# First layer's down projection: the last latent operands are split ahead of two closings, and the second layer's rows are loaded in other places

## The chip, the cores and the metric

One core of a Trainium2 chip runs the whole kernel. The metric is the device time of one execution in microseconds (us). Engine names in the profile: PE is the matrix engine (PEld its weight loads), DVE the vector engine, ACT the scalar engine, POOL GpSimd; SP only issues DMAs here, in a fixed order, and POOL issues the stores of results.

## The reference, cut to what matters

Two layers run over 1024 latent tokens and 256 context tokens, 1024 wide. Each layer has a mixer and a gated FFN with a convolution. The change lies where the FFN of the first layer ends and the mixer of the second begins:

```python
u = h @ w_up; u = conv3(u) + conv_b
a, g = jnp.split(u, 2, axis=-1)
y = (jax.nn.silu(g) * a) @ w_down            # 2816 x 1024, the "down projection"
x   = x   + g2  * rms_norm(y_lat, norm_post_ffn)      # "closing" of latent rows
ctx = ctx + g2c * rms_norm(y_ctx, norm_post_ffn)      # closing of context rows
...
h_lat = rms_norm(x, norm_pre_mix[1]) * (1.0 + sc1) + sh1   # second layer, mixer
qkv = h_lat @ w_qkv
```

## The kernel before, in words

Every float32 product is made of three matmuls on rounded halves: an operand is split by an ACT copy into a high part (`d_Ah`, `d_Bh`, line 1809) and by a DVE subtraction into a low part (`d_Al`, `d_Bl`, line 1810), and PE multiplies high by high, low by high, high by low (line 136, through the helper `mm`). A is the activation (`actd`), B the weight (`w_down`).

`ffn_down` (line 1750) runs in numbered steps `g`. Steps 0 to 41 are the latent tokens: seven products of a Strassen scheme, `P1, P5, P2, P3, P6, P4, P7`, of six chunks each (`NG` = 6, `NS` = 42; a chunk has 1024 columns, the sixth, that is step 41, only 512). P7 is special: at step 39 PE takes its last three chunks (steps 39, 40, 41) together, for one of the four result tiles after the other, so that all operands of steps 40 and 41 must be there soon after step 39 begins. For the first result tile these are 6 matmuls of step 39, 6 of step 40, then 3 of step 41. Steps 42 to 63 are the context tokens: one weight each, `k` = 0 to 21 (called weight 0 to 21 below), 512 KB each, 12 matmuls per weight; the last four weights, 18 to 21, are multiplied together at step 60. The activation of the context comes in pieces of four weights, the last piece is half as large (256 KB, with weight 20). Steps up to 71 follow without products.

In each step the program writes the products, then `prepare` (the operands of later steps: `prep`, and the loads of still later ones: `loads`), then the entries of `todo` for that step, and from step 42 on one `next(other)`. At step 39 (`last`) `prepare` comes first. This written order is the order of each engine's queue; no scheduler reorders it. A queue stands still while its first instruction waits.

- For latent operands of P7, `prep` first corrects the weight on DVE (`total`, line 1814: `d_t<-d_rawB,d_t`), ACT makes the high parts, DVE the low ones.
- `todo` holds the closings. `add(y2..)` adds a result bank to a saved tile (`p1`, line 1937: `y<-d_ps,d_p`). `leave(i)` closes 128 latent rows: two multiplications (line 1959), two additions of the old rows (line 1937: `y<-y,y_x`), two stores to `x2d` (POOL, line 1963). Latent tiles 4 to 7 are closed by `leave(4)` to `leave(7)` at steps 45, 47, 49, 51, with one store each (line 1965).
- `other` is the generator `odd_early` (line 2145): from a certain step on it writes one row load of the second layer per step (`odd_load`, line 2128: `n_x<-x2d`, 512 KB on SP; row tiles 0 to 7 below) and, from the third load on, one step of `odd_norm` for row tiles 0 to 3: a square with sum on ACT (line 2137), a power on POOL, a scaling on DVE (line 2140). A row tile gathers 8 tokens from each of 16 grid rows, so it needs every latent tile to be stored. First load: step 56; last: step 63.
- A weight's load (`d_rawB<-in_w_down`, line 1775, SP) goes to one of three buffers; weight k waits until weight k - 3 is split. At step g the load of weight g - 36 is written, just ahead of that step's `next(other)`.

After step 71 come the two context closings (`out`, `leave(8)`, `leave(9)`), then `odd_values` of the second layer (transposes of the rows, line 2190, and the first products `g_ps`); its weight loads (`w_raw<-in_w_qkv`, line 2170) stand on SP behind the row loads.

Of the kernel before, what the change touches and what calls it, by code (L numbers as in the profile page):

```python
# [65 lines left out]
class Trunk:  # L66
# [1683 lines left out]
    def ffn_down(self, l, ctx, x_src, x_dst, hp, sp, pp, tp, beside=None):  # L1750
# [9 lines left out]
        NG = (H + 1) // 2  # L1760
        width = lambda c: min(2, H - 2 * c)

        def tile(pool, tag, name, n=1024, dtype=F32, bufs=1):
            return pool.tile([P, n], dtype, name=name, tag=tag, bufs=bufs)
# [165 lines left out]
        def at(g, f):  # L1930
            todo.setdefault(g, []).append(f)

        def square(src, ms, h):
            nc.scalar.activation(junk, src, AF.Square, scale=1.0 / 32.0, accum_out=ms[:, h:h + 1])

        def add(out, x, y):
            nc.vector.tensor_tensor(out=out, in0=x, in1=y, op=OP.add)
# [3 lines left out]
        def fetch_x(key, r):  # L1941
            pool, tags = [(sp, ("f_t0",)), (sp, ("f_t1",))][key % 2] if key not in (4, 5) else \
                (sp, [("w_S1h", "w_S1l"), ("w_S2h", "w_S2l")][key - 4])
            if len(tags) == 1:
                x = tile(pool, tags[0], "y_x", NTOK if ctx else SEQ)
                st["x", key] = [x[:, 512 * h:512 * h + 512] for h in range(2)]
                nc.sync.dma_start(x[:, :D], x_src(r))
            else:
                st["x", key] = [tile(pool, t, "y_x", 512) for t in tags]
                for h, x in enumerate(st["x", key]):  # L1950
                    nc.sync.dma_start(x, x_src(r)[:, 512 * h:512 * h + 512])

        def scale(key, ms):
            st["r", key] = self.y_rstd(ms)

        def leave(key, halves, kind, r, whole=None):

            for h, y in enumerate(halves):
                nc.vector.scalar_tensor_tensor(out=y, in0=y, scalar=st["r", key], in1=gates[kind][h], op0=OP.mult, op1=OP.mult)
            for h, (y, x) in enumerate(zip(halves, st.pop(("x", key)))):  # L1960
                add(y, y, x)
                if whole is None:
                    nc.gpsimd.dma_start(x_dst(r)[:, 512 * h:512 * h + 512], y)
            if whole is not None:
                nc.gpsimd.dma_start(x_dst(r), whole)
# [20 lines left out]
        Y = [y01[:, :512], y01[:, 512:], y23[:, :512], y23[:, 512:]]  # L1986
# [4 lines left out]
        p1 = [tile(sp, "w_" + t, "d_p1", 512) for t in ("S1h", "S1l", "S2h", "S2l")]  # L1991
        y1a = [tile(self.wp, "w_" + t, "y", 512) for t in ("A12h", "A12l", "A21h", "A21l")]
        y1b = [tile(p, "w_" + t, "y", 512) for p, t in ((self.wp, "A22h"), (self.wp, "A22l"), (sp, "S3h"), (sp, "S3l"))]
        y2 = [tile(hp, "x_T4" + x, "y") for x in ("0h", "0l", "1h", "1l")]
        ms1, ms2 = ([self.small.tile([P, 2], F32, name=f"y_ms{j}", bufs=4) for _ in range(4)] for j in range(2))
        for i in range(4):
            at(NG + 1 + i, lambda i=i: nc.scalar.copy(p1[i], X[i]))
            at(2 * NG + 1 + i, lambda i=i: add(y2[i][:, 512:], Y[i], p1[i]))
            at(3 * NG + 1 + i, lambda i=i: (nc.scalar.copy(y1a[i], X[i]), square(X[i], ms1[i], 0)))
            at(4 * NG + 1 + i, lambda i=i: add(y1b[i], Y[i], p1[i]))  # L2000
            at(5 * NG + 1 + i, lambda i=i: add(y1b[i], X[i], y1b[i]))
            at(5 * NG + 2 + i, lambda i=i: square(y1b[i], ms1[i], 1))
            at(5 * NG + 3 + i, lambda i=i: scale(i, ms1[i]))
            at(6 * NG + 1 + i // 2 * (1 if ctx else 2), lambda i=i: add(y2[i][:, :512], Y[i], p1[i]))
        for i, (g, g1) in enumerate(((25, 34), (26, 35), (36, 38 if ctx else 39), (37, 39))):
            at(g, lambda i=i: fetch_x(i, i * P))
            at(g1, lambda i=i: leave(i, (y1a[i], y1b[i]), 0, i * P))
        r2 = lambda i: SEQ // 2 + i * P
# [54 lines left out]
        for i in range(5 if ctx else 0):  # L2063
            g = 6 * NG + 7 + 2 * i
# [80 lines left out]
    def odd_early(self, nx, junk):  # L2145

        self.odd_x = {}
        for _ in range(14):
            yield
        norm = self.odd_norm(range(4), junk)  # L2150
        for i in range(8):
            self.odd_load(nx, i)
            if i >= 2:
                next(norm)
            yield

    def odd_values(self, nx, gp, tp, sp):

# [643 lines left out]
```

## Time and profile before

| | us |
|---|---|
| runs before: median (lowest, highest of 3) | 3343.87 (3343.53, 3350.19) |
| the profiled execution: time | 3345.86 |
| the profiled execution: span of its instructions | 3344.1 |
| around the span | 1.8 |
| PE busy in the span | 3105.4 (93%) |
| mean granted clock of PE | 0.967 |

All times of the trace count from the start of the span. The down projection of the first layer lies between about 1675 and 1966 us, and the place of the change between 1870 and 1975 us. In a timeline row the first number is the start, the second the duration, then engine, line, operation and tiles; the bracket tells how long the engine was idle before it and what it waited for. A row of DMA issue tells when SP or POOL issued, not when the data landed; when a load landed is seen where an engine waited for it. Matmuls overlap, so a row of 0.39 us is followed by the next start 0.227 us later.

### The profile page before, as it was taken

To read this page: it belongs to the slowest core of one execution; us is meant where nothing else is said; L and a number is where in the kernel's file an instruction comes from. 1 tells how busy PE (TensorE), PEld (TensorE's weight loads), DVE (VectorE), ACT (ScalarE), POOL (GpSimd) and SP (SyncE) were. 2 spreads that over 40 slices of the span, in tenths; PEclk is the share of its full clock that TensorE was granted. 3 is DMA by queue.
4 is the path that set the end of the run, shared out by engine and by line. 5 is a ranking of instruction groups with operands and counts; after the bars stand their busy time and mean duration, and the time that the engine had idled before them with its cause. 6 is when DMAs were issued, how large, how long until landed. Compare 5 with 4: busy or idle time off the path is not lost.

```text
span 3344.1 us, 48796 instructions
## 1 busy us (share of the span) xinstructions
PE 3105.4 (93%) x18364; PEld 2555.0 (76%) x18364; DVE 2023.0 (60%) x3399; ACT 1501.9 (45%) x2681; POOL 1555.5 (47%) x1178
## 2 busy tenths in 40 slices
PE   7989998779998799999999989999998989999997
PEld 4766776658887688888878768889986768888785
DVE  4356666667775755455477863477775565545778
ACT  3222222266665544334344442466665534434443
POOL 1130111197774476666510111577774367777202
PEclk8999999889999899999999989999998989999998
DMA  6534333231113221122285772222224222222856
GB/s 247 195 90 138 123 120 115 88 97 45 59 67 126 71 72 66 70 74 70 80 297 191 256 242 105 79 65 62 61 74 161 85 69 76 88 82 82 277 182 220
DMA packets 202684, 398.73 MB, mean 119 GB/s; under 512 B 23360, under 2 KB 84800, under 8 KB 202448
## 3 DMA queue, kind: packets, MB, share of 16 engines
q1 hardware_dynamic: 191968, 358.91, 32.2%
q0 software_dynamic: 10480, 36.71, 2.9%
q8 instruction: 144, 2.36, 0.3%
q14 instruction: 92, 0.75, 0.1%
HBM read 316.86 MB, written 79.06 MB: 118 GB/s over the span
## 4 chain that ended last, share of the span: by engine, by line
PE 72%; DVE 10%; ACT 3%; issue 3%; DMA 3%; POOL 2%; SPq 0%; POOLq 0%; DVEq 0%; ACTq 0%
PE g_ps L136 18%; PE u_g L136 14%; PE u_v L136 10%; PE d_ps L136 10%; PE u_pc L136 4%; PE a_pv L136 2%; PE c_pv L136 2%; PE c_s L136 2%; PE c_pt L2437 2%; PE a_pt L1080 2%; DVE a_pl L1082 1%; PE o_ps L136 1%; PE a_s L136 1%; PE mod_ps L136 1%; ACT a_ph L1081 1%
## 5 line engine op out<-in xcount | busy, mean ns | idle before, releaser
L144 POOL TENSOR_TENSOR rs_r<-rs_e,mhalf 128x1 f32<-128x1 f32 (+3 forms) x106 | 82.2, 776 | 929.9 <-DVE rs_e L143 877.1
L136 PE MATMUL d_ps<-d_Bh,d_Ah 128*128 128x512 f32 x704 | 276.1, 392 | 7.4 <-ACT d_Bh L1809 7.3
L136 PE MATMUL d_ps<-d_Bl,d_Ah 128*128 128x512 f32 x704 | 276.7, 393 | 3.5 <-DVE d_Bl L1810 3.1
L136 PE MATMUL d_ps<-d_Bh,d_Al 128*128 128x512 f32 x704 | 275.9, 392 | 1.6 <-DVE d_Al L1810 1.6
L2420 POOL TENSOR_SCALAR c_p<-c_p,rl 128x640 f32<-128x640 f32 (+1 forms) x128 | 232.6, 1818 | 95.9 <-DVE rl L2419 63.7
L1060 POOL TENSOR_SCALAR a_p<-a_p,rl 128x1280 f32<-128x1280 f32 (+1 forms) x80 | 240.4, 3010 | 54.3 <-DVE rl L1059 47.1
L136 PE MATMUL g_ps<-xh,w_hi 128*128 128x512 f32 (+1 forms) x640 | 258.2, 403 | 3.6 <-DVE hq L711 2.2
L136 PE MATMUL g_ps<-xh,w_lo 128*128 128x512 f32 (+1 forms) x640 | 238.9, 373 | 0.9 <-POOL w_lo L2320 0.9
L136 PE MATMUL g_ps<-xl,w_hi 128*128 128x512 f32 (+1 forms) x640 | 239.1, 374 | 0.0
L1082 DVE TENSOR_TENSOR a_pl<-a_pt,a_ph 128x512 fp32r<-128x512 f32 (+1 forms) x200 | 119.0, 603 | 91.7 <-ACT a_ph L1081 91.6
L1497 DVE TENSOR_TENSOR f_u<-u_v,f_p 128x512 f32<-128x512 f32 x88 | 60.5, 688 | 186.2 <-PE u_v L136 186.2
L1483 POOL TENSOR_TENSOR w_S4l<-w_s,w_S4h 128x512 fp32r<-128x512 f32 x44 | 57.2, 1300 | 231.1 <-ACT w_S4h L1482 231.1
L136 PEld LDWEIGHTS d_ps<-d_Bh,d_Ah 128*128 128x128 f32 x704 | 133.1, 189 | 37.0 <-ACT d_Bh L1809 8.2
L136 PEld LDWEIGHTS d_ps<-d_Bl,d_Ah 128*128 128x128 f32 x704 | 133.1, 189 | 35.2 <-DVE d_Bl L1810 7.2
L136 PEld LDWEIGHTS d_ps<-d_Bh,d_Al 128*128 128x128 f32 x704 | 132.9, 189 | 30.1 <-DVE d_Al L1810 3.0
L136 PEld LDWEIGHTS g_ps<-xh,w_hi 128*128 128x128 f32 x640 | 122.6, 192 | 42.6 <-issue 27.7
L1081 ACT CAST a_ph<-a_pt 128x512 fp32r<-128x512 f32 (+1 forms) x200 | 101.9, 518 | 107.2 <-PE a_pt L1080 107.1
L136 PE MATMUL g_ps<-w_hi,xh 128*128 128x512 f32 (+1 forms) x368 | 144.2, 392 | 4.8 <-DVE xh L2194 2.1
L2440 DVE TENSOR_TENSOR c_pl<-c_pt,c_ph 128x256 fp32r<-128x256 f32 (+1 forms) x256 | 113.0, 470 | 58.3 <-ACT c_ph L2439 57.1
L136 PE MATMUL g_ps<-w_lo,xh 128*128 128x512 f32 (+1 forms) x368 | 137.9, 375 | 4.1 <-DVE w_lo L2181 2.9
L136 PEld LDWEIGHTS g_ps<-xh,w_lo 128*128 128x128 f32 x640 | 122.1, 191 | 23.9 <-POOL w_lo L2320 1.3
L2439 ACT CAST c_ph<-c_pt 128x256 fp32r<-128x256 f32 (+1 forms) x256 | 98.4, 414 | 91.2 <-PE c_pt L2437 89.1
(546 smaller groups left out, 9901.1 us busy)
## 6 DMA issues: line engine op xcount, KB each, us to landing
m_raw<-in_w_mod SPq DMA_DIRECT2D x96, 512.0 KB
w_raw<-in_w_up SPq DMA_DIRECT2D x88, 512.0 KB
d_rawA<-actd SPq DMA_DIRECT2D x77, 512.0 KB
d_rawB<-in_w_down SPq DMA_DIRECT2D x74, 512.0 KB
actd<-f_t SPq DMA_DIRECT2D x22, 640.0 KB
d_t<-in_w_down SPq DMA_DIRECT2D x22, 512.0 KB
actd<-f_t SPq DMA_DIRECT2D x22, 512.0 KB
d_s<-actd SPq DMA_DIRECT2D x20, 512.0 KB
```

The costliest lines, as they stand in the source:

```text
L136: return self.nc.tensor.matmul(out, lhsT, rhs, start=start, stop=stop, skip_group_check=True, **k)
L144: nc.gpsimd.tensor_tensor(out=r[:p, :n], in0=e[:p, :n], in1=self.mhalf[:p, :n], op=OP.pow)
L1060: nc.gpsimd.tensor_scalar(Pt[:, :nk], Pt[:, :nk], rl, None, op0=OP.mult)
L1080: nc.tensor.transpose(pt[:, m, qt * P:(qt + 1) * P], Pt[:, kts[j + m] * P:(kts[j + m] + 1) * P], self.ident)
L1081: nc.scalar.copy(ph[:, j:j + n], pt[:, :n])
L1082: nc.vector.tensor_tensor(out=pl[:, j:j + n], in0=pt[:, :n], in1=ph[:, j:j + n].bitcast(F32), op=OP.subtract)
L1483: nc.gpsimd.tensor_tensor(out=lo, in0=part(j, name), in1=hi.bitcast(F32), op=OP.subtract)
L1497: nc.vector.tensor_tensor(out=out, in0=x, in1=y, op=OP.add)
L2420: nc.gpsimd.tensor_scalar(Pt[:, :n], Pt[:, :n], rl, None, op0=OP.mult)
L2437: nc.tensor.transpose(pt[:, j, :], Pt[:, (src + j) * P:(src + j + 1) * P], self.ident)
L2439: nc.scalar.copy(vap(ph, o, dims), pt[:, :cnt])
L2440: nc.vector.tensor_tensor(out=vap(pl, o, dims), in0=pt[:, :cnt], in1=vap(ph, o, dims).bitcast(F32), op=OP.subtract)
```

## The change

```diff
-            at(6 * NG + 1 + i // 2 * (1 if ctx else 2), lambda i=i: add(y2[i][:, :512], Y[i], p1[i]))
-        for i, (g, g1) in enumerate(((25, 34), (26, 35), (36, 38 if ctx else 39), (37, 39))):
+            at(6 * NG + 1 + i // 2 * 2, lambda i=i: add(y2[i][:, :512], Y[i], p1[i]))
+        for i, (g, g1) in enumerate(((25, 34), (26, 35), (36, 39), (37, 39))):
...
-        for _ in range(14):
+        for _ in range(11):
             yield
         norm = self.odd_norm(range(4), junk)
         for i in range(8):
             self.odd_load(nx, i)
             if i >= 2:
                 next(norm)
             yield
+            if i < 6:
+                yield
```

`ctx` is true in the first layer alone; in the second layer nothing changes. In the first, two `add(y2..)` and `leave(2)` go from step 38 to step 39, where `prepare` stands ahead of `todo`. The row loads go from steps 56 to 63 to steps 53, 55, 57, 59, 61, 63, 65 and 66, and the norm's steps with the last six of them. No instruction is added or taken away.

On DVE, at the end of the latent products (`d_t`, `d_Al`, `d_Bl` with 512 columns are the operands of step 41; `y<-d_ps,d_p` the adds; the two multiplications with a gate and the `y<-y,y_x` pair behind them one `leave`). Before, from the last operand of step 40 on:

```order
L1810 TENSOR_TENSOR d_Bl<-d_t,d_Bh 128x1024
L1937 TENSOR_TENSOR y<-d_ps,d_p_16002 128x512
L1937 TENSOR_TENSOR y<-d_ps,d_p_16003 128x512
L1959 SCALAR_TENSOR_TENSOR y<-y,rs_r,gate_15996 128x512
L1959 SCALAR_TENSOR_TENSOR y<-y,rs_r,gate_15997 128x512
L1937 TENSOR_TENSOR y<-y,y_x 128x512 x2
L1814 TENSOR_TENSOR d_t<-d_rawB,d_t 128x512
L1810 TENSOR_TENSOR d_Al<-d_s,d_Ah 128x512
L1810 TENSOR_TENSOR d_Bl<-d_t,d_Bh 128x512
```

With the change, the same place:

```order
L1810 TENSOR_TENSOR d_Bl<-d_t,d_Bh 128x1024
L1814 TENSOR_TENSOR d_t<-d_rawB,d_t 128x512
L1810 TENSOR_TENSOR d_Al<-d_s,d_Ah 128x512
L1810 TENSOR_TENSOR d_Bl<-d_t,d_Bh 128x512
L1937 TENSOR_TENSOR y<-d_ps,d_p_16002 128x512
L1937 TENSOR_TENSOR y<-d_ps,d_p_16003 128x512
L1959 SCALAR_TENSOR_TENSOR y<-y,rs_r,gate_15996 128x512
L1959 SCALAR_TENSOR_TENSOR y<-y,rs_r,gate_15997 128x512
L1937 TENSOR_TENSOR y<-y,y_x 128x512 x2
```

The three operations of step 41 now stand ahead of the two adds and of `leave(2)`; `leave(3)`, which followed them before, stands behind all of it still. On POOL the order is the same as before.

On SP, at the last context weights (`d_rawB` with `x4` are weights 17 to 20 in the line taken out, `d_rawA` the last half-size piece, `n_x` the row loads):

```order
 L1775 DMA d_rawA<-actd 128x4x256
-L1775 DMA d_rawB<-in_w_down 128x1024 x4
-L1775 DMA d_rawA<-actd 128x2x256
+L1775 DMA d_rawB<-in_w_down 128x1024
+L2128 DMA n_x<-x2d 128x1x1024
+L1775 DMA d_rawB<-in_w_down 128x1024 x2
 L2128 DMA n_x<-x2d 128x1x1024
 L1775 DMA d_rawB<-in_w_down 128x1024
-L2128 DMA n_x<-x2d 128x1x1024 x3
+L1775 DMA d_rawA<-actd 128x2x256
+L1775 DMA d_rawB<-in_w_down 128x1024
+L2128 DMA n_x<-x2d 128x1x1024 x2
```

Before, one row load (row tile 0) stood ahead of weight 21, the last; now row tile 0 stands behind weight 17 and row tile 1 behind weight 19, so two stand ahead of weights 20 and 21. Row tiles 2 to 7 stay behind weight 21.

On ACT, at the same place (`d_Bh` are weights, `d_Ah` with 512 columns the last piece, `junk` the square of a row tile):

```order
 L1809 CAST d_Ah<-d_rawA 128x1024
-L1809 CAST d_Bh<-d_rawB 128x1024 x4
+L1809 CAST d_Bh<-d_rawB 128x1024 x3
+L2137 ACTIVATE junk,ms<-n_x 128x1024
+L1809 CAST d_Bh<-d_rawB 128x1024
 L1809 CAST d_Ah<-d_rawA 128x512
-L2137 ACTIVATE junk,ms<-n_x 128x1024
 L1809 CAST d_Bh<-d_rawB 128x1024
 L2137 ACTIVATE junk,ms<-n_x 128x1024 x3
```

The square of row tile 0 moved from between weights 20 and 21 to between weights 19 and 20.

## The prediction

> **What bounds the kernel now.** I read the page first, then PE's timeline at the two places that the change touches, then the queues that PE waits for there.
>
> ```profile
> span 3344.1 us, 48796 instructions
> PE 3105.4 (93%) x18364; PEld 2555.0 (76%) x18364; DVE 2023.0 (60%) x3399; ACT 1501.9 (45%) x2681; POOL 1555.5 (47%) x1178
> PE 72%; DVE 10%; ACT 3%; issue 3%; DMA 3%; POOL 2%; SPq 0%; POOLq 0%; DVEq 0%; ACTq 0%
> ```
>
> PE is busy for 93% of the span and makes 72% of the chain that ended last. So what takes away PE's idle time comes off the whole, as long as nothing behind it has to wait longer. PE stands still twice where the change acts. The first time is step 39, on PE's timeline:
>
> ```profile
> 1876.01 0.39 PE L136 MATMUL d_ps<-d_Bh,d_Al 128*128 128x512 f32 x1
> 1879.45 0.49 PE L136 MATMUL d_ps<-d_Bh,d_Ah 128*128 128x512 f32 x1 [3.05 <-ACT d_Bh L1809]
> 1880.17 0.50 PE L136 MATMUL d_ps<-d_Bl,d_Ah 128*128 128x512 f32 x1 [0.23 <-DVE d_Bl L1810]
> ...
> 1884.62 0.39 PE L136 MATMUL d_ps<-d_Bl,d_Ah 128*128 128x512 f32 x1
> 1884.85 0.39 PE L136 MATMUL d_ps<-d_Bh,d_Al 128*128 128x512 f32 x1
> ```
>
> Undisturbed starts are 0.227 us apart (1884.62 to 1884.85). The first matmul on step 41's operands should have started at 1876.24 and started at 1879.45. The reason stands in the DVE and ACT timelines:
>
> ```profile
> 1873.06 1.23 DVE L1810 TENSOR_TENSOR d_Bl<-d_t,d_Bh 128x1024 fp32r<-128x1024 f32 x1
> 1874.20 1.28 DVE L1937 TENSOR_TENSOR y<-d_ps,d_p 128x512 f32<-128x512 f32 x2
> 1875.40 1.41 DVE L1959 SCALAR_TENSOR_TENSOR y<-y,rs_r,gate 128x512 f32<-128x512 f32 x2
> 1876.72 1.28 DVE L1937 TENSOR_TENSOR y<-y,y_x 128x512 f32<-128x512 f32 x2
> 1877.93 0.68 DVE L1814 TENSOR_TENSOR d_t<-d_rawB,d_t 128x512 f32<-128x512 f32 x1
> 1879.43 0.69 DVE L1810 TENSOR_TENSOR d_Bl<-d_t,d_Bh 128x512 fp32r<-128x512 f32 x1 [0.22 <-ACT d_Bh L1809]
> ```
>
> ```profile
> 1873.53 0.62 ACT L1809 CAST d_Ah<-d_s 128x512 fp32r<-128x512 f32 x1 [0.50 <-PE d_ps L136]
> 1878.78 0.62 ACT L1809 CAST d_Bh<-d_t 128x512 fp32r<-128x512 f32 x1 [4.62 <-DVE d_t L1814]
> 1890.78 1.05 ACT L1809 CAST d_Bh<-d_rawB 128x1024 fp32r<-128x1024 f32 x1 [11.39 <-PE d_ps L136]
> ```
>
> DVE works without a break, but from 1874.20 to 1877.93, for 3.73 us, on the two adds and `leave(2)`, which nobody needs yet; `d_t` waits behind them, ACT idles 4.62 us for `d_t`, PE for ACT.
>
> The second standstill is step 60, the last four context weights. PE, then ACT, whose casts start when their loads land:
>
> ```profile
> 1949.49 0.50 PE L136 MATMUL d_ps<-d_Bh,d_Al 128*128 128x512 f32 x1
> 1954.23 0.80 PE L136 MATMUL d_ps<-d_Bh,d_Ah 128*128 128x512 f32 x1 [4.23 <-ACT d_Bh L1809]
> 1971.02 1.97 PE L2190 MATMUL n_pt<-ident,n_x 128*128 128x128 f32 x8 [4.25 <-DVE y L2103]
> ```
>
> ```profile
> 1940.62 1.05 ACT L1809 CAST d_Bh<-d_rawB 128x1024 fp32r<-128x1024 f32 x1 [3.19 <-DMA d_rawB<-in_w_down]
> 1941.91 1.05 ACT L1809 CAST d_Bh<-d_rawB 128x1024 fp32r<-128x1024 f32 x1 [0.24 <-DMA d_rawB<-in_w_down]
> 1943.15 1.05 ACT L1809 CAST d_Bh<-d_rawB 128x1024 fp32r<-128x1024 f32 x1 [0.19 <-DMA d_rawB<-in_w_down]
> 1946.52 1.05 ACT L1809 CAST d_Bh<-d_rawB 128x1024 fp32r<-128x1024 f32 x1 [2.32 <-DMA d_rawB<-in_w_down]
> 1950.98 1.06 ACT L2137 ACTIVATE junk<-n_x 128x1024 bf16<-128x1024 f32 x1 [2.89 <-DMA n_x<-x2d]
> 1953.13 1.04 ACT L1809 CAST d_Bh<-d_rawB 128x1024 fp32r<-128x1024 f32 x1 [1.00 <-DMA d_rawB<-in_w_down]
> 1955.16 1.06 ACT L2137 ACTIVATE junk<-n_x 128x1024 bf16<-128x1024 f32 x1 [0.99 <-DMA n_x<-x2d]
> 1957.21 1.06 ACT L2137 ACTIVATE junk<-n_x 128x1024 bf16<-128x1024 f32 x1 [0.90 <-DMA n_x<-x2d]
> ```
>
> These are weights 17, 18, 19, 20, row tile 0, weight 21, row tiles 1 and 2, in the order in which they landed. PE's second standstill ends with weight 21, and weight 21 landed behind a row tile. All that follows (context closings, transposes at 1971.02) hangs on it.
>
> **First part: the closings step back.** It adds no work. The adds and `leave(2)` now follow step 41's operands. `d_t` starts at 1874.20 instead of 1877.93, 3.73 earlier; the cast follows as before 0.85 later (1877.93 to 1878.78), at 1875.05; `d_Bl` 0.65 after that, at 1875.70. PE took the cast 0.67 after its start and `d_Bl` 0.74 after its start; so they are ready at 1875.72 and 1876.44, and PE wants them at 1876.24 and 1876.47. The standstill is gone, the second operand with almost nothing to spare. What it is worth:
>
> ```profile
> 1879.40:1884.60 5.20, 4.92 (x13) 3.69 (x14) 3.22 (x5) 0.00 (x0) 1.08 (x2) 0.67 0.69 231
> ```
>
> This row (columns: length, PE, PEld, DVE, ACT, POOL, granted clock, DMA share, GB/s) counts 13 matmuls from 1879.45 on, at a clock of 0.67; the fourteenth starts at 1884.62. Undisturbed it starts at 1876.24 + 13 x 0.227 = 1879.19. The gain is 5.43: 3.21 until the first matmul, 0.49 at the second (0.72 instead of 0.227), 1.73 on the slow stretch behind the standstill.
>
> Who pays? Behind the moved work on DVE stands `leave(3)`, and all three end at the same time as before, because the sum of the work is the same; the next DVE work, the first context weight, waits for a cast that PE releases only at 1890.78 (5.4 earlier now, 1885.4), while DVE is done by about 1882.6. The two stores of `leave(2)` leave POOL some 2 us later, but the first reader of `x2d` is over 50 us away. The banks that the adds free are PE's next at step 42, which follows 10 us on. From 1890.78 on every engine is released by PE, so all of it shifts by 5.4.
>
> The page "TensorE: Matmul & The Clock Gate" of the Trainium skill (section "HAM oscillation — how this bites in real kernels") warns of idle gaps of PE above about 3.4 us; by it a gap of 3.05 would leave the clock alone, and the first part would be worth 3.70 only. The trace has 0.67 right behind this gap, so I keep the whole.
>
> **Second part: the rows go ahead of the last weights.** Now SP, and the store that the rows wait for:
>
> ```profile
> 1936.12 0.33 SPq L1775 DMA_DIRECT2D d_rawB<-in_w_down  x1
> 1937.26 1.46 SPq L1775 DMA_DIRECT2D d_rawB<-in_w_down  x2
> 1942.96 0.33 SPq L1775 DMA_DIRECT2D d_rawB<-in_w_down  x1
> 1944.06 0.58 SPq L2128 DMA_DIRECT2D n_x<-x2d  x1
> 1944.73 0.53 SPq L1775 DMA_DIRECT2D d_rawB<-in_w_down  x1
> ```
>
> ```profile
> 1935.26 0.57 POOL L1965 DMA_DIRECT2D x2d<-y  x1 [2.95 <-DVE y L1937]
> ```
>
> ```profile
> x2d<-y POOLq DMA_DIRECT2D x1, 512.0 KB, 3.2
> ```
>
> ```profile
> 1942.00:1944.50 2.50, 2.50 (x13) 2.07 (x12) 2.42 (x3) 2.02 (x2) 0.00 (x0) 1.00 0.33 82
> ```
>
> In the clock of before: row tile 0's load is next behind weight 17 (1936.12), and waits for `leave(7)`'s store, 1935.26 + 3.2 = 1938.5. Queued behind it on SP are weights 18 and 19, which go out at about 1939.2 instead of 1937.26, then row tile 1. Nothing runs dry by that: weight 17 lands only at 1940.62. Weight 20 still goes out at 1942.96, since its buffer is weight 17's. What was a hole (the DMA engines busy 0.33 of 1942.0 to 1944.5) is filled with row data. In return two row tiles instead of one land ahead of weight 21.
>
> Prices: a weight behind a weight takes 1.29 or 1.24 (1940.62, 1941.91, 1943.15); a row tile behind another load 2.03 and 2.05 (1953.13, 1955.16, 1957.21); a weight behind a row tile 2.15 (1950.98 to 1953.13); the half-size piece half a weight, 0.65. After weight 17 come row tile 0, weight 18, weight 19, row tile 1, weight 20, the piece, weight 21. Lower end, rows 2.05 and each weight 1.29: 1940.62 + 4.1 + 5.16 + 0.65 = 1950.5, 2.6 earlier than 1953.13. Upper end: row tile 0 itself took from 1946.52 to 1950.98, less the piece 3.81; two rows at that and the three weights next to a row (18, 20, 21) at 2.15: 1940.62 + 7.62 + 6.45 + 1.24 + 0.65 = 1956.6, 3.5 later. I take rows at 2.05, the price seen twice, and those three weights at 2.15, as the trace shows them between rows: 1940.62 + 4.1 + 6.45 + 1.24 + 0.65 = 1953.06, that is -0.1. So the hole that is filled and the row that comes ahead cancel.
>
> The page "DMA: Bandwidth & Descriptors" of the Trainium skill (section "Anatomy of one DMA — SWDGE (gpsimd) path") makes the moving part bytes / 436 GB/s, an estimate of 1.2 us for 512 KB whatever the rows; by it weight 21 would come at or before the lower end. Weights agree (1.24), row tiles do not (2.05), so the measured prices stand.
>
> PE reaches weights 18 to 20 about 1947 and waits in pieces rather than once, but restarts with weight 21 as before; I leave its slow restart as it is. The square of row tile 0, now between weights 19 and 20 on ACT, costs nothing, since ACT idles 2.32 there. The later norm steps lie beside step 60's products.
>
> **Sum.** -5.4 - 0.1 = -5.5. The profiled execution took 3345.86 (span 3344.1 and 1.8 around it): 3340.4. It stood 2.0 above the median, and the difference applies to the median as well: 3343.87 - 5.5 = **3338.4**.
>
> **Rivals.** (1) *The rows hide in the hole*: the lower end, -2.6 more, 3335.8; a shorter standstill could save up to half of the slow restart as well:
>
> ```profile
> 1954.20:1966.40 12.20, 11.71 (x42) 0.78 1.03 262
> ```
>
> 39 matmuls stand from 1954.23 to the end, 8.9 us undisturbed in a stretch of 12.2, so 3.3 at most. For it: the hole is there. Against: weight 21 took 2.15 between rows. (2) *The rows hold the weights up*: the upper end, +3.5, 3341.9; for it speaks the 3.81 of row tile 0. (3) *The slow stretch at 1881 is not owed to the gap*: the first part gives 5.43 - 1.73 = 3.70, total -3.8, 3340.1. The 0.67 right behind the gap speaks against it. By the page "TensorE: Matmul & The Clock Gate" of the Trainium skill it would go this way. (4) *Slower*: SP stands at the head of row tile 0. If the store of `leave(7)` takes twice its 3.2, row tile 0 goes out at 1941.7, 3.2 later, with weights 18 and 19 behind it and the DMA engines dry; with rows at 3.81 that is +3.5 and +3.2, total -5.4 + 6.7 = +1.3, 3345.2. It decides from the point where weight 21 lands over 5.4 later relative to weight 17 than before. Against it: the trace's stores land in 3.2.
>
> **How the numbers follow.** Forecast 0.50 (its own range 3336.9 to 3340.0), rival 1 0.27, rival 2 0.13, rival 3 0.06, rival 4 0.04. The range reaches from the lower end with the whole 3.3 of the restart, 3332.5, to the upper end, 3341.9, and the 0.34 by which the two nearest runs before differ (3343.53 and 3343.87): 3342.3. A measurement here can tell about 0.2%, 6.7 us: faster means below 3337.2. That is nine tenths of rival 1 and a third of the forecast: 0.24 + 0.17 = 0.41; slower by 6.7 would need rival 4 twice over, 0.03; the same 0.56.
>
> **What would show it.** First part: no wait of PE for `d_Bh` on the 512-column operand, no clock below 1.00 before step 42, the first context cast some 5.4 earlier. Second: the cast of weight 21 as far behind that of weight 17 as before (12.5), the hole gone, row loads on SP behind weights 17 and 19. Wrong I would be if `d_Bl` came late at step 41 all the same, or if the distance from weight 17 to 21 moved by over 2 us.

## The result, and the profile after

Twenty executions of each kernel: the changed one takes 3338.89 us in the median (3335.14 to 3342.76), the kernel before 3346.14 (3338.43 to 3352.65). The ratio is 0.998 with a 95% interval of 0.9974 to 0.9986, that is 6.7 us less (4.7 to 8.7; by the ratio). The forecast was 5.5 us less, 3338.4. The profiled execution of the changed kernel took 3340.86. Lines after `odd_early` have numbers higher by 2.

The page's span, busy and chain rows:

```profile
span 3339.1 us, 48796 instructions
PE 3105.0 (93%) x18364; PEld 2556.2 (77%) x18364; DVE 2023.8 (61%) x3399; ACT 1502.0 (45%) x2681; POOL 1554.4 (47%) x1178
PE 74%; DVE 9%; ACT 3%; issue 3%; DMA 2%; POOL 1%; SPq 0%; POOLq 0%; DVEq 0%; ACTq 0%
```

No engine has less to do; the span is 5.0 shorter, which is waiting. In this execution the work ahead of the change runs 2.16 later than in the one of before (the last `d_Bl` of step 40 starts at 1875.22 instead of 1873.06), so below I compare distances, not clock times. DVE, then ACT, at step 39:

```profile
1875.22 1.22 DVE L1810 TENSOR_TENSOR d_Bl<-d_t,d_Bh 128x1024 fp32r<-128x1024 f32 x1
1876.36 0.68 DVE L1814 TENSOR_TENSOR d_t<-d_rawB,d_t 128x512 f32<-128x512 f32 x1
1876.96 0.68 DVE L1810 TENSOR_TENSOR d_Al<-d_s,d_Ah 128x512 fp32r<-128x512 f32 x1
1877.87 0.69 DVE L1810 TENSOR_TENSOR d_Bl<-d_t,d_Bh 128x512 fp32r<-128x512 f32 x1 [0.22 <-ACT d_Bh L1809]
1878.47 1.28 DVE L1937 TENSOR_TENSOR y<-d_ps,d_p 128x512 f32<-128x512 f32 x2
```

```profile
1877.21 0.62 ACT L1809 CAST d_Bh<-d_t 128x512 fp32r<-128x512 f32 x1 [0.89 <-DVE d_t L1814]
1887.60 1.05 ACT L1809 CAST d_Bh<-d_rawB 128x1024 fp32r<-128x1024 f32 x1 [9.77 <-PE d_ps L136]
```

`d_t` now follows `d_Bl` at once, and ACT's idle time before the cast is 0.89 instead of 4.62. PE, where the bracket of 3.05 was:

```profile
1878.40 0.39 PE L136 MATMUL d_ps<-d_Bh,d_Ah 128*128 128x512 f32 x1
1878.63 0.49 PE L136 MATMUL d_ps<-d_Bl,d_Ah 128*128 128x512 f32 x1
1878.95 0.40 PE L136 MATMUL d_ps<-d_Bh,d_Al 128*128 128x512 f32 x1
```

There is no bracket left, only a start 0.32 after its neighbour instead of 0.227, where `d_Bl` came just in time. The stretch behind, in the view by stretches, is at full clock:

```profile
1881.00:1884.40 3.40, 3.40 (x16) 2.82 (x15) 3.40 (x7) 0.00 (x0) 1.12 (x2) 1.00 0.36 131
```

Now step 60, ACT (weights 17, 18, 19, row tile 0, weights 20 and 21), PE and SP:

```profile
1937.20 1.05 ACT L1809 CAST d_Bh<-d_rawB 128x1024 fp32r<-128x1024 f32 x1 [2.56 <-DMA d_rawB<-in_w_down]
1941.85 1.05 ACT L1809 CAST d_Bh<-d_rawB 128x1024 fp32r<-128x1024 f32 x1 [3.60 <-DMA d_rawB<-in_w_down]
1943.59 1.05 ACT L1809 CAST d_Bh<-d_rawB 128x1024 fp32r<-128x1024 f32 x1 [0.69 <-DMA d_rawB<-in_w_down]
1944.54 1.05 ACT L2137 ACTIVATE junk<-n_x 128x1024 bf16<-128x1024 f32 x1
1946.91 1.04 ACT L1809 CAST d_Bh<-d_rawB 128x1024 fp32r<-128x1024 f32 x1 [1.22 <-DMA d_rawB<-in_w_down]
1949.39 1.05 ACT L1809 CAST d_Bh<-d_rawB 128x1024 fp32r<-128x1024 f32 x1 [0.92 <-DMA d_rawB<-in_w_down]
```

```profile
1945.95 0.50 PE L136 MATMUL d_ps<-d_Bl,d_Ah 128*128 128x512 f32 x1 [0.77 <-DVE d_Bl L1810]
1948.52 0.50 PE L136 MATMUL d_ps<-d_Bh,d_Ah 128*128 128x512 f32 x1 [1.85 <-ACT d_Ah L1809]
1949.27 0.50 PE L136 MATMUL d_ps<-d_Bl,d_Ah 128*128 128x512 f32 x1 [0.24 <-DVE d_Bl L1810]
1951.75 0.80 PE L136 MATMUL d_ps<-d_Bl,d_Ah 128*128 128x512 f32 x1 [0.66 <-DVE rs_e L143]
1968.06 1.97 PE L2192 MATMUL n_pt<-ident,n_x 128*128 128x128 f32 x8 [4.25 <-DVE y L2103]
1972.10 0.77 PE L136 MATMUL g_ps<-w_hi,xh 128*128 128x512 f32 x1 [2.08 <-DVE xh L2196]
```

```profile
1933.26 0.33 SPq L1775 DMA_DIRECT2D d_rawB<-in_w_down  x1
1935.77 0.58 SPq L2128 DMA_DIRECT2D n_x<-x2d  x1
1936.46 1.00 SPq L1775 DMA_DIRECT2D d_rawB<-in_w_down  x2
1937.51 0.56 SPq L2128 DMA_DIRECT2D n_x<-x2d  x1
1939.54 0.33 SPq L1775 DMA_DIRECT2D d_rawB<-in_w_down  x1
```

The rows do go out behind weights 17 and 19, and the hole is filled. Before, it lay 1.4 to 3.9 us behind the cast of weight 17, with a DMA share (the last number but one) of 0.33. The same stretch now, behind the cast at 1937.20:

```profile
1938.60:1941.10 2.50, 2.50 (x12) 2.07 (x11) 0.91 (x1) 0.00 (x0) 0.00 (x0) 1.00 1.02 305
```

A smaller hole has opened just ahead of it, behind the late start of row tile 0 (1935.77):

```profile
1936.50:1938.00 1.50, 1.50 (x9) 1.23 (x8) 0.14 (x1) 0.80 (x1) 0.00 (x0) 1.00 0.65 150
```

Weight 21 comes 12.19 behind weight 17, where before it came 12.51 behind. PE's waits of step 60, one of 4.23 and two short ones before (0.21, 0.47), have become four of 3.52 together, and behind them the half clock is the same: 0.50 over 6.6 and 6.7 us (before, then after).

```profile
1952.90:1959.50 6.60, 4.81 (x11) 3.43 (x12) 3.08 (x7) 3.34 (x5) 1.66 (x3) 0.50 1.03 236
```

```profile
1950.80:1957.50 6.70, 6.04 (x15) 4.54 (x15) 3.77 (x9) 2.99 (x6) 2.20 (x4) 0.50 1.03 293
```

### The profile page after: what moved, and what is told of

It is laid out like the page before. It is cut to its first block, busy times and chain, and to the rows that moved or that the text cites. A ratio compares the mean times of both kernels' runs of the same rounds, so it can differ in the third digit from the quotient of the medians.

```text
span 3339.1 us, 48796 instructions
## 1 busy us (share of the span) xinstructions
PE 3105.0 (93%) x18364; PEld 2556.2 (77%) x18364; DVE 2023.8 (61%) x3399; ACT 1502.0 (45%) x2681; POOL 1554.4 (47%) x1178
## 4 chain that ended last, share of the span: by engine, by line
PE 74%; DVE 9%; ACT 3%; issue 3%; DMA 2%; POOL 1%; SPq 0%; POOLq 0%; DVEq 0%; ACTq 0%
PE g_ps L136 18%; PE u_g L136 14%; PE d_ps L136 12%; PE u_v L136 10%; PE u_pc L136 4%; PE a_pv L136 2%; PE c_pv L136 2%; PE c_s L136 2%; PE a_pt L1080 2%; PE c_pt L2439 2%; DVE a_pl L1082 1%; PE o_ps L136 1%; PE a_s L136 1%; PE mod_ps L136 1%; ACT a_ph L1081 1%
```

## The experiments

Executions of one kernel scatter by up to 9 us to either side of the median, and 9 to 33 of them give a ratio good to about 3 us. So besides the time I read four distances from each trace: from the last `d_Bl` of step 40 to the first context cast, on to the cast of weight 17, on to that of weight 21, on to the second layer's first product (`g_ps`). All in us, one execution a row. The three traces of before differ by up to 1.3 us in a column, so a smaller difference between two single traces means little.

| kernel | to first context cast | to weight 17 | to weight 21 | to first product | together |
|---|---|---|---|---|---|
| before | 17.72 | 49.84 | 12.51 | 21.94 | 102.01 |
| same_gap_again_1 (before) | 18.47 | 50.43 | 11.47 | 22.12 | 102.49 |
| same_gap_again_2 (before) | 17.75 | 51.01 | 12.79 | 21.39 | 102.94 |
| after | 12.38 | 49.60 | 12.19 | 22.71 | 96.88 |
| first_part_alone | 12.40 | 50.49 | 12.11 | 22.83 | 97.83 |
| second_part_alone | 16.09 | 50.08 | 12.08 | 21.43 | 99.68 |
| adds_ahead_only | 13.58 | 50.25 | 12.61 | 22.10 | 98.54 |
| three_closings_ahead | 20.21 | 51.54 | 10.75 | 21.66 | 104.16 |
| four_rows_ahead | 12.38 | 50.06 | 17.05 | 22.02 | 101.51 |
| no_row_ahead_of_the_weights | 12.38 | 50.18 | 10.15 | 23.66 | 96.37 |
| rows_in_a_block | 12.41 | 51.00 | 10.20 | 21.96 | 95.57 |
| closing_rows_into_the_hole | 12.38 | 50.23 | 9.57 | 23.01 | 95.19 |
| late_rows_behind_first_weight | 12.36 | 51.17 | 10.72 | 21.57 | 95.82 |

### The first part alone

Both lines with `ctx` changed, `odd_early` as before.

> Only the closings step back; the row loads stand as before (row tile 0 ahead of weight 21, none behind weights 17 and 19). Theory (the DVE queue ahead of step 41's operands is the cause, the slow clock behind the gap belongs to it, and the second part is worth nothing): 5.4 us faster than before, no wait of the matrix engine at step 39, no clock below 1.00 there, and from the cast of weight 17 to that of weight 21 12.5 us as before. Rival (the rows hide in the hole): the first part gives 5.4, the changed kernel is 2.6 or more faster than this one. Rival (the slow stretch is not owed to the gap): 3.7 faster, a clock near 0.5 somewhere between step 39 and step 42.

3340.32 against 3346.19, ratio 0.9985 (0.9976 to 0.9995): 5.0 less (1.7 to 8.0). The standstill of step 39 is gone (12.40), the second keeps its single wait:

```profile
1950.22 0.50 PE L136 MATMUL d_ps<-d_Bh,d_Ah 128*128 128x512 f32 x1 [3.72 <-ACT d_Bh L1809]
```

### The second part alone

Only `odd_early` changed.

> Only the row loads are moved; the closings stand as before. Theory: no difference to before within what can be measured (-0.1 us), the wait of 3.05 us at step 39 and the clock of about 0.67 behind it are there, weight 17 to weight 21 takes 12.2 to 12.5 us. Rival (the rows hide in the hole): 2.6 us faster, weight 17 to weight 21 in 9.9 us. Rival (the rows hold the weights up): 3.5 us slower, 16.0 us.

3346.75 against 3346.19, ratio 1.0003 (0.9994 to 1.0012): nothing that can be measured (2.0 less to 4.0 more, which excludes the 2.6 less of rival 1). The 6.7 of both parts and the 5.0 of the first alone don't differ by more than the scatter either. The wait of step 39 is there to the digit, but the clock behind it is not slow this time:

```profile
1880.53 0.50 PE L136 MATMUL d_ps<-d_Bh,d_Ah 128*128 128x512 f32 x1 [3.05 <-ACT d_Bh L1809]
```

```profile
1880.90:1884.30 3.40, 3.17 (x14) 2.55 (x14) 2.83 (x5) 0.00 (x0) 0.81 (x2) 1.00 0.75 216
```

So the same gap cost 16.09 - 12.38 = 3.71 here, where before's trace had 5.34. This is rival 3's price, in a kernel whose step 39 is the one of before.

### The same gap in further executions

The kernel before, unchanged, twice.

> The kernel before, unchanged, for another trace of its standstill at step 39. One trace showed a slow stretch right behind the gap of 3.05 us (first context cast 17.72 us after the last d_Bl of step 40), the trace of the second part alone shows the same gap and a clock of 1.00 behind it. If the slow stretch hangs on where windows of about 3.41 us that start by a clock of their own fall on the gap, further traces show it some times and not others, with the first context cast at 17.7 with it and about 16.0 without. If the gap always brings it and the second part had taken it away, it is here again, 17.7.

> The kernel before, unchanged, once more. By windows of their own clock: 17.7 with a slow stretch or 16.0 without, from execution to execution. By the gap alone: 17.7 each time.

The gap is 3.05 and 3.06, the first context cast comes after 18.47 and 17.75. Granted clock (last number but two) in the first, then in the second:

```profile
1875.00:1878.40 3.40, 1.18 (x6) 0.64 (x4) 3.40 (x7) 0.00 (x0) 0.89 (x2) 0.97 0.33 127
1878.50:1885.20 6.70, 5.97 (x14) 4.43 (x15) 3.71 (x6) 0.62 (x1) 1.21 (x3) 0.51 0.65 235
1885.30:1888.70 3.40, 3.40 (x16) 2.77 (x16) 0.00 (x0) 0.00 (x0) 0.00 (x0) 1.00 0.02 5
```

```profile
1882.10:1885.40 3.30, 3.30 (x9) 2.57 (x8) 1.22 (x3) 0.00 (x0) 1.08 (x2) 0.50 0.66 258
```

In the first the clock falls at 1878.2, before PE has even started again (1879.23), and stays low for two lengths of 3.4 us; in the second it falls 2 us after the restart (1880.12), for one. So the clock is low for none, one, one and two lengths in the four traces with the gap, and at 1.00 here in all eight without a gap of that size (12.36 to 13.58 in the first column). The gap brings it, but not every time. The places lie on a grid that the kernel doesn't set: before's granted clock, read in slices of 0.2 to 0.3 us, changes at 1881.12, 1884.54, 1952.80 and 1959.63, that is 1, 21 and 23 lengths of 3.413 us behind the first, and the other traces have the same spacing with another start. The Trainium skill, page "TensorE: Matmul & The Clock Gate", section "What's actually happening", says that activity is judged in free-running windows of 3413 ns, and this spacing agrees. What makes a window slow was not found: by the grid of its own trace the second part alone had 1.8 us of the gap in one window and kept its clock, while the second trace here lost it behind a window with 1.5. Nor is the share of such executions known from four traces.

### One closing more ahead of the operands

Before, with `leave(3)` at step 38 as well.

```diff
-(36, 38 if ctx else 39), (37, 39)
+(36, 38 if ctx else 39), (37, 38 if ctx else 39)
```

> The kernel before with the closing of latent tile 3 moved from step 39 to step 38 too, so that the vector engine has one more closing (2.53 us of work) ahead of step 41's operands. Theory (the vector engine's queue alone sets the wait at step 39): the matrix engine waits 5.6 us there instead of 3.05, and the kernel is 2.5 us slower than before, up to 4.2 if one more clock period at half speed is lost. Rival (the wait has another end, a load or a bank): the wait stays near 3.05 and nothing changes.

3348.03 against 3344.20, ratio 1.0010 (1.0001 to 1.0019): 3.3 more (0.3 to 6.4), where 2.5 to 4.2 was expected. The wait grows by the length of one `leave` (2.53), as a queue demands:

```profile
1879.72 0.79 PE L136 MATMUL d_ps<-d_Bh,d_Ah 128*128 128x512 f32 x1 [5.58 <-ACT d_Bh L1809]
```

The clock is low for two lengths of 3.4 us here, from 1877.1, again before PE restarts.

### Only the adds ahead

Before, with `leave(2)` alone moved to step 39.

```diff
-(36, 38 if ctx else 39), (37, 39)
+(36, 39), (37, 39)
```

> The kernel before, with leave(2) alone moved behind step 41's operands; the two adds stay ahead of them, the row loads stay as before. If the head of the DVE queue sets the standstill of step 39, each us ahead of d_t counts once: the adds take 1.20 us (1874.20 to 1875.40 in the trace of before), so the first operand is there 1.20 later than without them, 1876.92 where PE wants it at 1876.24: a wait of PE of about 0.7 for d_Bh, and about 0.5 in all at d_Bl, instead of 3.05 and 0.23. The rival, that it is leave(2) with its stores or its old rows and not the plain length of the queue, gives a wait of 0. On the clock: if a window goes slow only where PE stands still for over 1 us in it, none here shows 0.5 ahead of step 42.

```profile
1881.36 0.49 PE L136 MATMUL d_ps<-d_Bh,d_Ah 128*128 128x512 f32 x1 [0.52 <-ACT d_Bh L1809]
1882.09 0.50 PE L136 MATMUL d_ps<-d_Bl,d_Ah 128*128 128x512 f32 x1 [0.23 <-DVE d_Bl L1810]
```

The bracket of 0.52 is a start 0.68 late (1881.36, where the start before it, at 1880.45, would have been followed at 1880.68): the 0.7 that was expected. In all it is 13.58 - 12.40 = 1.18, as expected, and there is no slow stretch. A single execution each took 3346.30 and 3346.14, which tells nothing at this size. Zero, 1.20, 3.73 and 6.26 us of work ahead of `d_t` thus give brackets of none, 0.52, 3.05 and 5.58: the length of the queue less 0.68 each time, and no single operation in it.

### Four rows ahead of weight 21

After, without the second `yield`, so a row load behind every weight.

```diff
-            if i < 6:
-                yield
```

> The changed kernel with one row load in every step from step 53 on, so that four row tiles stand ahead of weight 21 instead of two. Theory on prices (2.05 us a row tile, 2.15 for a weight next to one, the hole filled only once): weight 17 to weight 21 takes 17.3 us instead of 12.2, and the kernel is 4 to 5 us slower than the changed kernel, about as slow as before. Rival (rows hide beside the weights): 12.2 us, no difference to the changed kernel.

17.05 from weight 17 to 21 (17.3 was worked out with the prediction's prices), and 3344.47, ratio 0.9995 (0.9986 to 1.0003): 1.7 less than before (4.7 less to 1.0 more), so most of the first part's gain is given back, as expected. So rows ahead of the last weight do cost, and what is on the path is weight 21.

### No row ahead of weight 21

The first part, with all row loads behind weight 21.

```diff
-        for _ in range(11):
+        for _ in range(15):
...
-            if i < 6:
-                yield
```

> The first part, and the first row load one step later than before, so that all eight row loads stand behind weight 21. Theory on prices: without a row tile in front weight 21 lands about 1.3 to 2.2 us behind the half-size piece, so weight 17 to weight 21 takes 8 to 9 us instead of 12.5, the matrix engine waits at most 1.5 us at step 60 and its clock stays at 1.00, so the context products end 7 us earlier than in the first part alone. How much of it reaches the end divides two views. If weight 21 alone is what the second layer waits for: 12 us faster than before in all. If the stream of loads is the next bound, with the second layer's first weight at its end: that weight lands as late as in the first part alone, behind the same eight row tiles, the first products of the second layer wait for it, and the whole is only 6 to 7 us faster than before.

10.15 instead of the 8 to 9 expected, and the time is that of the first part alone: 3340.52, ratio 0.9986 (0.9977 to 0.9995), 4.7 less, where 12 or 6 to 7 was expected. PE still waits 1.69 for weight 21, and its clock, expected at 1.00, is low for one length of 3.4 us from 1953.7 on. What is won at weight 21 is partly given back behind it. ACT:

```profile
1951.11 1.04 ACT L1809 CAST d_Bh<-d_rawB 128x1024 fp32r<-128x1024 f32 x1 [2.48 <-DMA d_rawB<-in_w_down]
...
1961.60 1.06 ACT L2137 ACTIVATE junk<-n_x 128x1024 bf16<-128x1024 f32 x1 [4.01 <-DMA n_x<-x2d]
...
1962.66 0.58 ACT L1934 ACTIVATE yjunk<-d_ps 128x512 f32<-128x512 f32 x1
```

Row tile 3's square stands on ACT ahead of the context closing (1962.66) and waits 4.01 for its rows; weight 21 to the first product is 23.66, where the first part alone has 22.83. The other view, that the second layer's weights at the end of the stream become the next bound, shows in the trace too (its chain holds a wait of 4.37 for `w_raw` up to 1977.45), so how much each costs is open. And weight 21 lands 4.05 behind weight 20, though only a half-size piece lies between. The row loads issued 0.6 behind it may share the DMA engines with it; but with the same eight behind it in `closing_rows_into_the_hole` below it lands 2.42 behind weight 20, so that stays open.

### Rows in one piece

After, with row tiles of 128 rows that lie together. They are other tokens than the reference asks for, and each waits for fewer stores, so the time is not one of the task; the trace is there for the price of a row tile.

```diff
-            src = self.x2d[0:SEQ].rearrange("(r g i) d -> g r i d", g=8, i=8)[i]
+            src = self.x2d[i * P:(i + 1) * P]
```

> The changed kernel, but a row tile of the second layer is 128 tokens that follow each other in memory instead of 8 tokens out of each of 16 grid rows; the bytes and the number of pieces are the same. It takes other tokens than the reference asks for and needs not wait for the last stores, so its time is no time of the task. If a row tile is dear because its 16 pieces of 32 KB lie 256 KB apart: it takes 1.3 us like a weight instead of 2.05, and weight 17 to weight 21 takes 8 to 9 us instead of 12.2. If it is dear for another reason (data just written, or the place that it is written to): 2.05 and about 12 as before.

```profile
1938.62 1.05 ACT L1809 CAST d_Bh<-d_rawB 128x1024 fp32r<-128x1024 f32 x1 [3.35 <-DMA d_rawB<-in_w_down]
1941.20 1.05 ACT L1809 CAST d_Bh<-d_rawB 128x1024 fp32r<-128x1024 f32 x1 [1.54 <-DMA d_rawB<-in_w_down]
1942.48 1.05 ACT L1809 CAST d_Bh<-d_rawB 128x1024 fp32r<-128x1024 f32 x1 [0.22 <-DMA d_rawB<-in_w_down]
```

Weight 18 comes 2.58 behind weight 17 with a row tile between them, that is 1.29 each if they share alike, where the gathered tile and weight took 4.65. Of the distance from 17 to 21, 2.0 go (12.19 to 10.20), not the 3 to 4 of the stronger view. But this distance mixes two things: row tile 0 went out 0.42 behind weight 17 here (1933.52 and 1933.94) and 2.51 behind it in the changed kernel (1933.26 and 1935.77), where it waited for a store. The pattern alone shows behind weight 21, where nothing waits for a store. First the changed kernel, then this one, each while row tiles 4 to 7 come in (by their order on SP):

```profile
1957.00:1963.00 6.00, 6.00 (x27) 4.92 (x26) 2.36 (x5) 1.38 (x4) 0.65 (x2) 0.95 1.03 242
```

```profile
1954.00:1957.00 3.00, 3.00 (x12) 2.44 (x11) 1.54 (x5) 0.37 (x1) 1.10 (x2) 0.77 1.02 408
```

With the DMA engines as busy (1.03 and 1.02), gathered rows move 242 GB/s and rows in one piece 408 (the last number), that is 2.17 and 1.29 us for 512 KB. Both are rows of `x2d` written shortly before, so it is the pattern (16 pieces at a stride of 256 KB) that makes a row tile dear, and not that its data is fresh. The Trainium skill, page "DMA: Bandwidth & Descriptors", section "Latency and other measured facts", has copies that slow down as the row pitch grows in powers of two, from 207 GB/s at 512 KiB to 103 at 4 MiB. It has no row for 256 KB, and its 207 is close to the 214 that it calls full, so it doesn't foretell the loss seen here. Time 3339.71, ratio 0.9983 (0.9973 to 0.9993).

### The closings' old rows into the hole

No row ahead of weight 21, and the loads of the context closings' old rows (`y_x<-x1d`), which lie together, at steps 53 and 54.

```diff
-            at(NS + NC - 4, lambda i=i: fetch_x(8 + i, SEQ + i * P))
+            at(NS + 11 + i, lambda i=i: fetch_x(8 + i, SEQ + i * P))
```

> As the run without a row ahead of the weights, but the two loads of old context rows for the closings, which cost about 1.3 us each, are issued behind weights 17 and 18, where the hole in the stream is, instead of between row tiles 2 and 3. Theory (in the run without rows ahead, the square of row tile 3 on the scalar engine held up the context closings behind it): weight 17 to weight 21 stays near 10.2 us, row tile 3 lands 3 us earlier, and the first product of the second layer comes 2.3 us earlier relative to weight 17 (31.5 instead of 33.8), so 7 us faster than before. Rival (the end of the context products alone counts, or the two loads hold weight 21 up by their 2.6 us): 4.7 us faster than before or less.

9.57 to weight 21, 95.19 in all, the shortest of the traces, and 3338.63 against 3344.20, ratio 0.9984 (0.9975 to 0.9993): 5.4 less, where 7 was expected. From weight 17 to the first product it is 32.58 (31.5 expected; 33.81 with no row ahead), and the square of row tile 3 starts 1.2 earlier behind weight 17, not 3, still with the closing right behind it. In its trace 1.7 is won on the changed kernel; the times can't tell the two apart.

### Late rows behind the second layer's first weight

The last kernel, with row tiles 4 to 7 loaded behind weight 0 of `w_qkv`.

```diff
-            self.odd_load(nx, i)
+            if i < 4:
+                self.odd_load(nx, i)
...
+                if m == 0:
+                    for i in range(4, 8):
+                        self.odd_load(nx, i)
```

> As the run with the closing rows in the hole, and row tiles 4 to 7, which the second layer needs 15 us later than row tiles 0 to 3, are loaded behind its first weight instead of ahead of it. If that weight, at the end of the stream of loads, holds up the first products: another 1 to 2 us faster than with the closing rows in the hole alone. If the context closings set the start of the first products: the same time.

3339.68, ratio 0.9985 (0.9977 to 0.9994), from weight 17 to the first product 32.29 instead of 32.58: 0.3 shorter, where 1 to 2 was expected if that weight held things up. That speaks against the order of these loads as what starts the second layer. The trace's chain runs through the context closings on DVE (`y`, up to 1967.99) into the first product's operand, which fits the other view.

## Why the prediction was right

**The DVE queue (first part).** Right. The wait of 3.05 is gone, alone 5.0 are won, and the doses of work above (1.20, 3.73 and 6.26) show that it is the length of the queue. "The second operand with almost nothing to spare" held: the prediction had 0.03 to spare, the trace a start 0.09 late (0.32 for 0.227).

**What it is worth: 5.43.** Between these two executions 17.72 - 12.38 = 5.34. But the term of 1.73 for the slow stretch was read from one execution and is not constant: the four traces with the gap give 16.09, 17.72, 17.75 and 18.47, so it cost 3.7 to 6.1, on their mean (17.51) 5.1. Rival 3 was set against the forecast as either-or; each is true in some executions. That the sum fits the median rests on a slow stretch being there in three of four, which the one execution read could not tell: here the prediction had luck. The rule that it quotes from the Trainium skill (page "TensorE: Matmul & The Clock Gate", section "HAM oscillation — how this bites in real kernels") warns only of gaps above about 3.4 us; a gap of 3.05 was enough in three of four traces.

**The rest of the step hidden.** Right: `leave(3)` and the stores cost nothing, and from the last `d_Bl` to the first context cast nothing new waits.

**The rows: -0.1.** Right in sum: 12.19 against 12.51, and alone ratio 1.0003. With the old order the six traces spread from 10.75 to 12.79 by themselves, so -0.3 is no gain, and 12.19 for the 12.44 worked out is closer than these traces can tell. The prices were less right than their sum: row tile 0 with weight 18 took 4.65 (4.20 worked out), weight 19 1.74 (1.24), row tile 1 with weight 20 3.32 (4.20), piece and weight 21 2.48 (2.80). A price per load is a mean here; over seven or nine loads the errors cancel, in `four_rows_ahead` too: 17.05 for 17.3. "Nothing runs dry" did not quite hold: the small hole around the cast of weight 17 (share 0.65) lies partly in the 4.65.

**The wait for the store, and the slow restart.** Right. Row tile 0's load went out at 1935.77; the store of `leave(7)` was issued at 1932.39 and should land 3.2 later, at 1935.6. Weights 18 and 19 stood behind it until 1936.46 while weight 17 was still under way. PE's waits come in pieces, and the half clock behind them lasts as long as before.

**The rivals.** Rival 1 fell: the rows do not hide (12.19), and even with no row ahead of it weight 21 came 9.57 to 10.72 behind weight 17, about what rival 1 hoped for with two rows ahead. Rivals 2 and 4 fell with 12.19, and SP's standstill stayed short.

**The sum.** -5.5 was forecast. From the last `d_Bl` to the first product it is 96.88 in the one trace of the changed kernel against a mean of 102.48 in three traces of before: -5.6. The measured 6.7 (4.7 to 8.7) holds both. That the time itself came within 0.5 (3338.89 for 3338.4) is luck in part: the median before was 3346.14, 2.3 above that of the three runs that the forecast started from, and the gain, 7.25 between the two medians, was 1.8 above the forecast.

## What to carry to other kernels

Where a written order is a queue's order, look at what stands ahead of the operand that the bounding engine waits for, and move what nobody needs yet behind it: its whole length comes back, less the slack, and no instruction has to get faster. Filling a hole in the DMA with data that then stands ahead of the last operand won nothing here; with cheaper data (in one piece) single traces were 1.3 and 1.7 us shorter, which the times did not confirm. A clock drop seen in one execution is to be priced from several.

## What the runs showed of the hardware

- A gap of PE of 3.05 us was followed by no, one or two stretches of about 3.4 us at half clock, in four executions of the same code ahead of it; the clock can fall while PE still stands (1878.2, restart at 1879.23). One of 0.52 us was followed by none, in one trace.
- The changes of the granted clock within a trace lie whole multiples of 3.413 us apart (before: 1, 21 and 23), and start elsewhere in each trace.
- 512 KB loads of 16 pieces at a stride of 256 KB moved 242 GB/s with the DMA engines fully busy, loads in one piece 408: 2.17 and 1.29 us, the latter the same as a weight.
- The last weight, with a half-size piece between it and weight 20, landed 2.42 to 4.05 us behind weight 20, with the same eight row loads issued behind it at both ends. What decides it was not found.
